# A hybrid decoder layer on one core: x loaded by columns, and the first transposes and splits ordered by k-tile

## The chip, the core and the metric

The kernel runs on one core of a Trainium2 chip. The metric is the device time of one execution in microseconds (us), the median of several runs. Times inside an execution come from a profile of one execution, counted from the start of its span.

Names of the engines: TensorE (PE, with its weight loads PEld), VectorE (DVE), ScalarE (ACT), GpSimd (POOL) and SyncE (SP), which issues most transfers.

## The reference

One decoder layer for 256 tokens with a width of 1024, all in float32: a SwiGLU feed-forward of width 2816 with RMSNorm before and after it, a mixer (state space branch and differential attention), and a second feed-forward. Only the beginning of the first feed-forward bears on the change:

```
def rmsnorm(x, g):
    y = x * lax.rsqrt(jnp.mean(x * x, axis=-1, keepdims=True) + EPS)
    return y * g

def swiglu(x, w_gate, w_up, w_down):
    return (silu(x @ w_gate) * (x @ w_up)) @ w_down

h = h + 0.5 * rmsnorm(swiglu(rmsnorm(h, ffn1_pre_g), ffn1_w_gate, ffn1_w_up, ffn1_w_down), ffn1_post_g)
```

## The kernel before, in words

Products keep close to float32 accuracy by splitting both operands into a rounded upper part (`hi`, type float32r) and a remainder (`lo`). ScalarE writes `hi` (a copy or an activation with a new type), VectorE writes `lo` as the difference, and TensorE sums three products: hi by hi, lo by hi, hi by lo.

The 256 tokens are two blocks of 128, the width of 1024 is eight k-tiles of 128. x lies in the tile `h` as 128 x 2 blocks x 1024. Weights come in chunks of 1 MB through three buffers called `raw`; each chunk is split into `whi` and `wlo`. The first four chunks hold 512 rows (four k-tiles) by 512 columns: two of `w_gate`, then two of `w_up`. The function `load_to` (line 231) issues the loads on SyncE's queue, the first chunk in four quarters of one k-tile each; a buffer is loaded again when its last split is done. `split_steps` (line 241) is a generator that issues the splits of a chunk piece by piece; the very first piece is copied by VectorE, the others by ScalarE. The first chunk's pieces are one k-tile each.

At the beginning there is no norm yet. `raised(b, q)` (line 888) transposes 512 columns (half q) of block b on TensorE, four transposes into one PSUM bank. `raw(b, q)` (line 891), through `gained` (line 473), writes hi and lo of the transposed columns times the norm's gain into the tile `raw_u` of that block and half: four activations on ScalarE, then four remainders on VectorE. The products are taken from these unnormed activations; the row factor `1 / rms` is applied later, when the sums are read. `square` (line 496) sums the squares for it, on VectorE for block 0 and on ScalarE for block 1.

`mm_both` (line 345) multiplies one chunk with both blocks: 24 products of 128 x 128 by 512 columns, six for each k-tile, in the order hi of k-tiles 0 and 1, lo of 0, hi of 2, lo of 1, hi of 3, lo of 2, lo of 3. Its argument `between` calls a function after so many products. In `first_products` (line 908) the first chunk's call puts the transposes of the second half behind products 10 and 14. The second chunk's call follows, then two more for `w_up`.

The order of TensorE, ScalarE, VectorE and SyncE is that in which the program issues the instructions here (`own_order`, line 387); each engine works its own list in order, and waits between engines are set by the tiles that are written and read. `warm(n)` (line 422) issues filler products on zeros; `FILL` is the number after the first transposes.

Order of the work before: SyncE loads block 0's first 512 columns of x, block 1's, the four quarters of the first chunk, the second 512 columns of both blocks, the second and third chunk. TensorE does five fillers, a small transpose of the gains, four transposes of block 0, a filler, four of block 1, two fillers, and the first products.

Of the kernel before, what the change touches and what calls it, by code (L numbers as in the profile page):

```python
# [16 lines left out]
F32 = mybir.dt.float32  # L17
F32R = mybir.dt.float32r
AF = mybir.ActivationFunctionType
ALU = mybir.AluOpType  # L20
# [6 lines left out]
P = 128  # L27
T = 256
# [10 lines left out]
RAW_BUFS = 3  # L39
H_PAD, ACS_PAD = 32, 0  # L40
AHEAD = 3
WARM = 5
FILL = 2
TAIL = 3
BG_US = 3.15
QK_US = 2.4
# [8 lines left out]
def tile_hybrid_layer(ctx: ExitStack, tc: tile.TileContext, x, ffn1_pre_g, ffn1_w_gate, ffn1_w_up,  # L55
# [4 lines left out]
    nc = tc.nc  # L60
# [28 lines left out]
    def bg(shape, name):  # L89
        return ps.tile(shape, F32, tag="bg", name=name, bufs=5)  # L90
# [137 lines left out]

    taken = [0]

    def load_to(n):
        while len(raws) < min(n, len(chunks)):
            i = len(raws)
            src, shape = chunks[i]
            r = sb.tile(shape, F32, tag="raw", name=f"raw{i}", bufs=RAW_BUFS)
            nj = shape[1] // 4 if i == 0 else shape[1] // 2 if i < 4 else shape[1]
            for j in range(0, shape[1], nj):
                nc.sync.dma_start(r[:, j:j + nj, :], src[:, j:j + nj, :])
            raws.append(r)

    def split_steps(ahead=True):


        i, _ = units[len(splits)]
        load_to(i + 1)
        r, shape = raws[i], chunks[i][1]
        nj = shape[1] // 2
        his, los = [], []
        splits.append((his, los))
        for q in range(2):  # L250
            hi = k4([P, nj, shape[2]], f"whi{i}{q}", F32R)
            lo = k4([P, nj, shape[2]], f"wlo{i}{q}", F32R)
            his.append(hi)
            los.append(lo)
            n = 1 if i == 0 else nj
            for j in range(0, nj, n):
                js = slice(j, j + n)
                copy = nc.scalar.copy if i + q + j else nc.vector.tensor_copy
                behind(copy(hi[:, js, :], r[:, q * nj + j:q * nj + j + n, :]), "cast")  # L259
                if not i + q + j:  # L260
                    yield
                m = nc.vector.tensor_sub(lo[:, js, :], r[:, q * nj + j:q * nj + j + n, :], hi[:, js, :].bitcast(F32))  # L262
                last_wlo[0] = behind(m, "lo").ins
                yield
        raws[i] = None
        if ahead:
            load_to(i + 1 + RAW_BUFS)
# [79 lines left out]
    def mm_both(accs, w, acts, k0, first, last, between={}):  # L347


        wh, wl = w  # L350
        his = [[(b, a, wh, j) for b in range(2) for a in acts[b]] for j in range(4)]
        los = [[(b, acts[b][0], wl, j) for b in range(2)] for j in range(4)]
        terms = his[0] + his[1] + los[0] + his[2] + los[1] + his[3] + los[2] + los[3]
        for i, (b, x_, w_, j) in enumerate(terms):
            nc.tensor.matmul(accs[b], x_(k0 + j), w_(j), start=first and j == 0 and w_ is wh and x_ is acts[b][0],  # L355
                             stop=last and j == 3 and w_ is wl)
            if i + 1 in between:
                between[i + 1]()
# [39 lines left out]
    h = const.tile([P, 2, D], F32, name="h")  # L398
    xv = x[0].rearrange("(b p) d -> p b d", p=P)
    halves = (slice(0, 512), slice(512, D))  # L400
    for q in range(2):
        for b in range(2):
            nc.sync.dma_start(h[:, b, halves[q]], xv[:, b, halves[q]])
        load_to((1, RAW_BUFS)[q])
    act_table(SILU)

    zeros = const.tile([P, P], F32, name="zeros")
# [1 line left out]
    ident = const.tile([P, P], F32, name="ident")  # L409
# [41 lines left out]
    uh, ul, _ = act_u  # L451
# [15 lines left out]
    def transposed(b, q, src, name):  # L467
        pu = bg([P, 4, P], f"pu_{name}{b}{q}")
        for i in range(4):
            nc.tensor.transpose(pu[:, i, :], src[:, i * P:(i + 1) * P], ident)  # L470
        return pu

    def gained(pu, q, g, hi, lo):

        for i in range(4):
            nc.scalar.activation(hi[:, i, :], pu[:, i, :], AF.Identity, scale=g(q * 4 + i))
        for i in range(4):
            nc.vector.scalar_tensor_tensor(lo[:, i, :], pu[:, i, :], g(q * 4 + i), hi[:, i, :].bitcast(F32),
                                           ALU.mult, ALU.subtract)
# [16 lines left out]
    def square(ss, b, q, tag, eng=None):  # L496

        src = h[:, b, halves[q]]
        if eng is nc.vector:
            nc.vector.scalar_tensor_tensor(jk([P, 512], f"sq_{tag}{b}{q}"), src, 1.0 / D, src, ALU.mult,  # L500
                                           ALU.mult, accum_out=ss[:, q:q + 1])
        else:
            sum_sq(ss[:, q:q + 1], src, 1.0, f"sq_{tag}{b}{q}")
# [26 lines left out]
    def rescaled(pus, rbs, g, tag):  # L530

        out = []
        for q in range(2):
            us = k2([P, 4, P], f"us_{tag}{q}")
            for i in range(4):
                nc.vector.scalar_tensor_tensor(us[:, i, :], pus[q][:, i, :], g(q * 4 + i), rbs, ALU.mult,
                                               ALU.mult)
# [195 lines left out]
    class Norm:  # L733
# [63 lines left out]

        def rescale(self):
            rbs = on_rows(bg([P, P], f"rb_{self.tag}"), diag(self.r0, self.tag), self.tag)
            set_u(0, rescaled(self.pus, rbs, self.g, self.tag))  # L800

    ov = out[0].rearrange("(b p) d -> p b d", p=P)

# [81 lines left out]
    pus = [[None] * 2 for _ in range(2)]  # L885
    ss_f = [tiny(2, f"ss_f{b}") for b in range(2)]

    def raised(b, q):
        pus[b][q] = transposed(b, q, h[:, b, halves[q]], "f1")

    def raw(b, q):
        gained(pus[b][q], q, gain_f, *raw_to[b](q))

    square(ss_f[0], 0, 0, "f1", nc.vector)
    raised(0, 0)
    warm(1)
    raised(1, 0)
    warm(FILL)
    steps = split_steps(False)
    next(steps)  # L900
    raw(0, 0)
    raw(1, 0)
    for _ in steps:
        pass
    square(ss_f[1], 1, 0, "f1")
    load_to(1 + RAW_BUFS)

    def first_products(evict, back):


        acts = [of_block(to) for to in raw_to]
        acc = [[pj(f"pn_f1{b}0") for b in range(2)], None]
        mm_both(acc[0], take(1), acts, 0, True, False, {10: lambda: raised(0, 1), 14: lambda: raised(1, 1)})
        square(ss_f[0], 0, 1, "f1", nc.vector)
        r = [rstd_of(ss_f[0], 1.0, "r_f10")]
        dr = diag(r[0], "f10")
        raw(0, 1)
        raw(1, 1)
        rb = bg([P, 2, P], "rb_f1")
        rbs = []  # L920
        w = take(1)
        square(ss_f[1], 1, 1, "f1")
        r.append(rstd_of(ss_f[1], 1.0, "r_f11"))
        dr1 = diag(r[1], "f11")
        us = []

        def second():
            rbs.append(on_rows(rb[:, 0, :], dr, "f10"))
            us.append(rescaled(pus[0], rbs[0], gain_f, "f10"))
# [10 lines left out]
        us = rescaled(pus[1], rbs[1], gain_f, "f11")  # L940
# [178 lines left out]
    for i in range(4):  # L1119
        acc = k2([P, 2, T], f"bc{i}")  # L1120
# [447 lines left out]
```

## Time and profile before

| what | value |
|---|---|
| median of 3 runs | 734.62 us (733.73 to 734.84) |
| span of the profiled execution | 732.0 us |
| TensorE busy | 724.0 us, 99% of the span |
| VectorE busy | 609.2 us, 83% |
| ScalarE busy | 475.3 us, 65% |
| transfers | 137.92 MB, mean 188 GB/s |

The page gives the span of the profiled execution, from the first instruction to the last; what lies around it is not in the profile, and the median of the runs is 2.62 us above the span. In the profile's rows a line such as L476 is a line of the kernel, `out<-in` names tiles with their buffer numbers left out, and a merged row (x4) gives the start of the first and the length until the end of the last. Instructions of one engine overlap a little, so that a group of four is shorter than four times the length of one.

### The profile page before, as it was taken

The numbers are of one execution on the slowest core, as the hardware profiler recorded it, in microseconds if no ns is written. First come the engines' busy times: TensorE is split into PE (matmuls) and PEld (weight loads), VectorE is DVE, ScalarE is ACT, GpSimd is POOL, SyncE is SP. The second block draws the span as 40 slices with busy tenths as digits, with TensorE's granted clock in tenths as the row PEclk, the third lists the DMA queues.
The fourth block names the chain that finished last, engine by engine and source line by source line (L and its number), as shares of the span: only waits on it lengthen the run. The fifth ranks groups of instructions, "written<-read, shape, count | busy, mean of one in ns | idle before, by whom it ended". The sixth has DMA issues, their size and how long they took to land.

```text
span 732.0 us, 10570 instructions
## 1 busy us (share of the span) xinstructions
PE 724.0 (99%) x4025; PEld 618.4 (84%) x4025; DVE 609.2 (83%) x948; ACT 475.3 (65%) x815; POOL 37.0 (5%) x66
## 2 busy tenths in 40 slices
PE   9999999999999999999999999999999999999996
PEld 7888888888878889999888888888888888888885
DVE  6978787999979999877996997784784878779995
ACT  6656566656867676869965577772663657566562
POOL 2800000000200000000000000000010000000000
PEclk9999999999999999999999999999999999999999
DMA  8874645467673647666564664475471664654541
GB/s 290 241 247 157 225 146 203 173 210 279 182 228 118 201 146 250 187 192 207 159 221 146 215 209 147 140 246 187 129 238 35 231 195 153 227 205 145 185 185 57
DMA packets 94210, 137.92 MB, mean 188 GB/s; under 512 B 2684, under 2 KB 68304, under 8 KB 94160
## 3 DMA queue, kind: packets, MB, share of 16 engines
q1 hardware_dynamic: 91488, 129.51, 53.1%
q0 software_dynamic: 2368, 7.22, 3.2%
q8 instruction: 31, 0.51, 0.3%
q10 hardware_dynamic: 304, 0.53, 0.2%
q14 instruction: 19, 0.16, 0.1%
HBM read 136.17 MB, written 1.08 MB: 188 GB/s over the span
## 4 chain that ended last, share of the span: by engine, by line
PE 99%; DVE 0%; ACT 0%; DVEq 0%; issue 0%; ACTq 0%
PE pup_f L326 9%; PE pg_f L326 9%; PE pws L345 6%; PE pgt L345 6%; PE acc_f1p L692 5%; PE acc_f2p L692 5%; PE pxs L326 4%; PE pg_f L325 4%; PE pup_f L325 4%; PE pn_f L355 3%; PE acc_mx L614 3%; PE pn_mx L345 3%; PE pn_f L345 3%; PE pwd L345 3%; PE acc_f1p L614 2%; PE acc_f2p L614 2%
## 5 line engine op out<-in xcount | busy, mean ns | idle before, releaser
L262 DVE TENSOR_TENSOR wlo<-raw,whi 128x1024 fp32r<-128x1024 f32 (+1 forms) x222 | 262.2, 1209 | 19.5 <-ACT whi L259 18.3
L259 ACT CAST whi<-raw 128x1024 fp32r<-128x1024 f32 (+1 forms) x221 | 222.8, 1043 | 12.8 <-PE psc L1255 2.5
L326 PE MATMUL pup_f<-u_f,whi 128*128 128x512 f32 x288 | 101.5, 396 | 0.0
L326 PE MATMUL pg_f<-u_f,whi 128*128 128x512 f32 x288 | 101.3, 396 | 0.0
L325 PE MATMUL pg_f<-u_f,wlo 128*128 128x256 f32 x252 | 70.6, 280 | 0.0
L325 PE MATMUL pup_f<-u_f,wlo 128*128 128x256 f32 x252 | 70.3, 279 | 0.0
L326 PEld LDWEIGHTS pup_f<-u_f,whi 128*128 128x128 f32 x288 | 52.9, 188 | 9.9
L326 PEld LDWEIGHTS pg_f<-u_f,whi 128*128 128x128 f32 x288 | 52.8, 188 | 9.7
L325 PEld LDWEIGHTS pg_f<-u_f,wlo 128*128 128x128 f32 x252 | 47.5, 189 | 1.7
L325 PEld LDWEIGHTS pup_f<-u_f,wlo 128*128 128x128 f32 x252 | 47.5, 189 | 1.6
L326 PE MATMUL pxs<-u_mx,whi 128*128 128x512 f32 x128 | 44.6, 397 | 0.0
L130 ACT CAST wqh<-wt 128x1024 fp32r<-128x1024 f32 x24 | 25.3, 1054 | 23.3 <-DVE wt L122 22.1
L330 ACT COPY su_f<-pup_f 128x256 f32<-128x256 f32 x36 | 13.4, 372 | 37.5 <-PE pup_f L326 37.4
L331 DVE TENSOR_TENSOR su_f<-pup_f,su_f 128x256 f32<-128x256 f32 x36 | 15.1, 421 | 25.0 <-ACT su_f L330 24.9
L345 PE MATMUL pgt<-whi,u_mx 128*128 128x512 f32 x128 | 33.1, 393 | 0.0
L311 PE MATMUL pz<-u_mx,whi 128*128 128x256 f32 x128 | 31.8, 285 | 0.0
L312 PE MATMUL pz<-u_mx,whi 128*128 128x256 f32 x128 | 31.4, 283 | 0.0
L325 PE MATMUL pxs<-u_mx,wlo 128*128 128x256 f32 x112 | 31.2, 279 | 0.0
L135 DVE TENSOR_TENSOR wql<-wt,wqh 128x1024 fp32r<-128x1024 f32 x24 | 29.2, 1218 | 0.2
L345 PEld LDWEIGHTS pgt<-whi,u_mx 128*128 128x128 f32 x128 | 23.6, 188 | 5.3 <-issue 0.7
L326 PEld LDWEIGHTS pxs<-u_mx,whi 128*128 128x128 f32 x128 | 23.2, 188 | 4.2
L301 ACT CAST gh_f<-sg_f 128x512 fp32r<-128x512 f32 x18 | 11.2, 620 | 23.0 <-DVE sg_f L848 23.0
(415 smaller groups left out, 1699.1 us busy)
## 6 DMA issues: line engine op xcount, KB each, us to landing
raw<-in_w_in_dram SPq DMA_DIRECT2D x40, 1024.0 KB, 5.2
raw<-in_ffn_w_down_dram SPq DMA_DIRECT2D x22, 1024.0 KB, 4.9
raw<-in_ffn_w_gate_dram SPq DMA_DIRECT2D x20, 1024.0 KB, 5.2
raw<-in_ffn_w_up_dram SPq DMA_DIRECT2D x20, 1024.0 KB, 5.2
raw<-in_ssd_w_branch_dram SPq DMA_DIRECT2D x8, 1024.0 KB, 4.9
acb<-acd POOLq DMA_DIRECT2D x8, 512.0 KB, 5.0
raw<-in_da_w_branch_dram SPq DMA_DIRECT2D x4, 1024.0 KB, 4.9
raw<-in_w_out_dram SPq DMA_DIRECT2D x4, 1024.0 KB, 4.9
```

Source lines behind the costliest of these rows:

```text
L130: nc.scalar.copy(hi, src)
L135: nc.vector.tensor_sub(lo, src, hi.bitcast(F32))
L259: behind(copy(hi[:, js, :], r[:, q * nj + j:q * nj + j + n, :]), "cast")
L262: m = nc.vector.tensor_sub(lo[:, js, :], r[:, q * nj + j:q * nj + j + n, :], hi[:, js, :].bitcast(F32))
L311: nc.tensor.matmul(acc[m], wh(j)[:, cs], ah(k0 + j), start=first and j == ks[0], stop=False)
L312: nc.tensor.matmul(acc[m], wh(j)[:, cs], al(k0 + j), start=False, stop=False)
L325: nc.tensor.matmul(acc[:, :T], wl(j)[:, cs], ah(j), start=False, stop=False)
L326: nc.tensor.matmul(acc, wh(j)[:, cs], ahl(j), start=j == 0, stop=j == KD - 1)
L345: nc.tensor.matmul(acc, a(k0 + j), b(j), start=first and i == 0, stop=last and i == 11)
L355: nc.tensor.matmul(accs[b], x_(k0 + j), w_(j), start=first and j == 0 and w_ is wh and x_ is acts[b][0], stop=last and j == 3 and w_ is wl)
L614: nc.tensor.matmul(acc[b][q][:, cs] if to is None else to, x_[:, ts], w_(kt)[:, halves[q]][:, cs], start=to is not None and kt == 0 and x_ ...
L692: nc.tensor.matmul(bank[p], x_, w_, start=p not in begun, stop=last and p in (1, 5, 6, 7))
```

## The change

x is loaded by columns: first 256 columns of both blocks in one transfer (`load_x`), then the first two quarters of the first weight chunk, then the next 256 columns of both blocks, then the other two quarters, then the rest of x by blocks as before. `load_to` has a callback for it.

`raised(n)` now transposes k-tiles 2n and 2n + 1 of both blocks (four transposes into one bank) and `raw(*ks)` writes hi and lo of whole k-tiles for both blocks. Before the first product stand the transposes of k-tiles 0 and 1 and one filler. The transposes of k-tiles 2 and 3, with their splits, the remaining splits of the first chunk and the first squares (`second_quarter`), are called after the sixth product. The transposes of k-tiles 4 and 5 and of 6 and 7 are called after products 16 and 20.

```
-FILL = 2
+FILL = 1
...
-    def load_to(n):
+    def load_to(n, half_way=None):
...
             for j in range(0, shape[1], nj):
+                if half_way is not None and j == shape[1] // 2:
+                    half_way()
                 nc.sync.dma_start(r[:, j:j + nj, :], src[:, j:j + nj, :])
...
-                if not i + q + j:
+                if i == 0:
                     yield
...
-    for q in range(2):
-        for b in range(2):
-            nc.sync.dma_start(h[:, b, halves[q]], xv[:, b, halves[q]])
-        load_to((1, RAW_BUFS)[q])
+    def load_x(cs):
+        nc.sync.dma_start(h[:, :, cs], xv[:, :, cs])
+
+    load_x(slice(0, T))
+    load_to(1, lambda: load_x(slice(T, 2 * T)))
+    for b in range(2):
+        nc.sync.dma_start(h[:, b, halves[1]], xv[:, b, halves[1]])
+    load_to(RAW_BUFS)
...
-    square(ss_f[0], 0, 0, "f1", nc.vector)
-    raised(0, 0)
-    warm(1)
-    raised(1, 0)
+    def raised(n):
+        pus[n] = pu = bg([P, 2, 2, P], f"pu_f1{n}")
+        for b in range(2):
+            for i in range(2):
+                nc.tensor.transpose(pu[:, b, i, :], h[:, b, (2 * n + i) * P:(2 * n + i + 1) * P], ident)
+
+    def raw(*ks):
+        for j in ks:
+            for b in range(2):
+                nc.scalar.activation(raw_to[b](j // 4)[0][:, j % 4, :], pus[j // 2][:, b, j % 2, :], AF.Identity,
+                                     scale=gain_f(j))
+        for j in ks:
+            for b in range(2):
+                hi, lo = raw_to[b](j // 4)
+                nc.vector.scalar_tensor_tensor(lo[:, j % 4, :], pus[j // 2][:, b, j % 2, :], gain_f(j),
+                                               hi[:, j % 4, :].bitcast(F32), ALU.mult, ALU.subtract)
+
+    raised(0)
     warm(FILL)
     steps = split_steps(False)
     next(steps)
-    raw(0, 0)
-    raw(1, 0)
-    for _ in steps:
-        pass
-    square(ss_f[1], 1, 0, "f1")
-    load_to(1 + RAW_BUFS)
+    raw(0)
+    raw(1)
+    next(steps)
+    next(steps)
+    next(steps)
+
+    def second_quarter():
+        raised(1)
+        next(steps)
+        raw(2)
+        next(steps)
+        next(steps)
+        raw(3)
+        for _ in steps:
+            pass
+        load_to(1 + RAW_BUFS)
+        square(ss_f[0], 0, 0, "f1", nc.vector)
+        square(ss_f[1], 1, 0, "f1")
...
-        mm_both(acc[0], take(1), acts, 0, True, False, {10: lambda: raised(0, 1), 14: lambda: raised(1, 1)})
+        mm_both(acc[0], take(1), acts, 0, True, False, {6: second_quarter, 16: lambda: raised(2), 20: lambda: raised(3)})
...
-        raw(0, 1)
-        raw(1, 1)
+        raw(4, 5)
+        raw(6, 7)
```

Two lines that rescale the transposed activations later (`rescaled`) take them by k-tile from the new banks; what they compute is the same.

More of the change, by code (lines that the diff above doesn't have):

```diff
@@ L535, in rescaled @@
             for i in range(4):
-                nc.vector.scalar_tensor_tensor(us[:, i, :], pus[q][:, i, :], g(q * 4 + i), rbs, ALU.mult,
+                nc.vector.scalar_tensor_tensor(us[:, i, :], pus[q][i], g(q * 4 + i), rbs, ALU.mult,
                                                ALU.mult)
@@ L799, in rescale @@
             rbs = on_rows(bg([P, P], f"rb_{self.tag}"), diag(self.r0, self.tag), self.tag)
-            set_u(0, rescaled(self.pus, rbs, self.g, self.tag))
+            set_u(0, rescaled([[pu[:, i, :] for i in range(4)] for pu in self.pus], rbs, self.g, self.tag))
     ov = out[0].rearrange("(b p) d -> p b d", p=P)
@@ L884, in tile_hybrid_layer, with of_pus @@
     gain_f = lambda j: cols_f[:, j:j + 1]
-    pus = [[None] * 2 for _ in range(2)]
+    pus = [None] * 4
     ss_f = [tiny(2, f"ss_f{b}") for b in range(2)]
[L888 to L892, printed above, removed]
-    square(ss_f[0], 0, 0, "f1", nc.vector)
-    raised(0, 0)
-    warm(1)
-    raised(1, 0)
+    def raised(n):
[3 more added lines that the diff above has]
+                nc.tensor.transpose(pu[:, b, i, :], h[:, b, (2 * n + i) * P:(2 * n + i + 1) * P], ident)
+    def of_pus(b):
+        return [[pus[2 * q + i // 2][:, b, i % 2, :] for i in range(4)] for q in range(2)]
+    def raw(*ks):
[9 more added lines that the diff above has]
+    raised(0)
     warm(FILL)
@@ L928, in second @@
             rbs.append(on_rows(rb[:, 0, :], dr, "f10"))
-            us.append(rescaled(pus[0], rbs[0], gain_f, "f10"))
+            us.append(rescaled(of_pus(0), rbs[0], gain_f, "f10"))
             ws.append(take(1))
@@ L939, in first_products @@
             evict(b, 0, acc[0][b], r[b])
-        us = rescaled(pus[1], rbs[1], gain_f, "f11")
+        us = rescaled(of_pus(1), rbs[1], gain_f, "f11")
         mm_both(acc[1], w2, acts, 0, True, False)
```

## The prediction

> **What bounds the kernel now.** I read the page first: its span, its busy times and the summary of the chain that ended last.
>
> ```profile
> span 732.0 us, 10570 instructions
> PE 724.0 (99%) x4025; PEld 618.4 (84%) x4025; DVE 609.2 (83%) x948; ACT 475.3 (65%) x815; POOL 37.0 (5%) x66
> PE 99%; DVE 0%; ACT 0%; DVEq 0%; issue 0%; ACTq 0%
> ```
>
> TensorE (PE) is busy for 724.0 of 732.0 us and the chain is TensorE nearly throughout. From the second weight chunk on, the compiled order of every engine is the same in both kernels. So what the change does to the time is what it does to the moment at which TensorE begins the second chunk's products; everything behind that moves along. The second view is the chain in order of time, at the beginning (start, length, what).
>
> ```profile
> 6.17 0.38 ACT raw_u L476
> 6.55 0.84 DVE raw_u L478 x3
> ...
> 7.59 0.35 DVE raw_u L478
> 7.98 2.10 PE pn_f L355 x7
> 10.09 0.44 PE pu_f L470 x4
> 10.52 0.93 PE pn_f L355 x4
> 11.46 0.44 PE pu_f L470 x4
> 11.89 4.29 PE pn_f L355 x18
> ```
>
> From 7.98 on the chain lies on TensorE. A product of 512 columns costs 0.93/4 = 0.233 us, four transposes 0.44. The first chunk has 24 products, six for each k-tile: four with the weights' upper part (`whi`), two with the remainder (`wlo`). I call them P1 to P24, and P25 is the second chunk's first. The third view is the timeline of the same stretch (start, length, engine, line, operation; in brackets the idle time and what ended it).
>
> ```profile
> 0.80 0.86 SPq L403 DMA_DIRECT2D h<-in_x_dram  x2
> 1.70 1.85 SPq L238 DMA_DIRECT2D raw<-in_ffn_w_gate_dram  x4
> 3.74 1.11 PE L470 MATMUL pu_f<-ident,h 128*128 128x128 f32 x4
> 4.89 2.43 ACT L476 ACTIVATE raw_u<-pu_f,cols_f 128x128 fp32r<-128x128 f32 x8 [2.20 <-PE pu_f L470]
> 5.08 1.06 PE L470 MATMUL pu_f<-ident,h 128*128 128x128 f32 x4
> 6.21 0.43 DVE L259 CAST whi<-raw 128x512 fp32r<-128x512 f32 x1 [1.59 <-DMA raw<-in_ffn_w_gate_dram]
> 6.55 2.15 DVE L478 SCALAR_TENSOR_TENSOR raw_u<-pu_f,cols_f,raw_u 128x128 fp32r<-128x128 f32 x8
> 6.78 0.94 PE L355 MATMUL pn_f<-whi,raw_u 128*128 128x512 f32 x3
> 7.19 1.68 ACT L259 CAST whi<-raw 128x512 fp32r<-128x512 f32 x3
> 7.98 1.42 PE L355 MATMUL pn_f<-whi,raw_u 128*128 128x512 f32 x5 [0.27 <-DVE raw_u L478]
> 8.62 2.49 DVE L262 TENSOR_TENSOR wlo<-raw,whi 128x512 fp32r<-128x512 f32 x4
> 9.36 0.73 PE L355 MATMUL pn_f<-wlo,raw_u 128*128 128x512 f32 x2
> 10.56 1.14 ACT L476 ACTIVATE raw_u<-pu_f,cols_f 128x128 fp32r<-128x128 f32 x4 [1.07 <-PE pu_f L470]
> 11.03 0.68 DVE L500 SCALAR_TENSOR_TENSOR sq_f<-h 128x512 f32<-128x512 f32 x1
> 11.93 1.14 ACT L476 ACTIVATE raw_u<-pu_f,cols_f 128x128 fp32r<-128x128 f32 x4 [0.23 <-PE pu_f L470]
> 12.95 2.01 ACT L259 CAST whi<-raw 128x1024 fp32r<-128x1024 f32 x2
> 13.11 1.12 DVE L478 SCALAR_TENSOR_TENSOR raw_u<-pu_f,cols_f,raw_u 128x128 fp32r<-128x128 f32 x4 [0.25 <-ACT raw_u L476]
> 14.06 1.69 PEld L355 LDWEIGHTS pn_f<-whi,raw_u 128*128 128x128 f32 x8 [0.29 <-ACT whi L259]
> 14.15 2.35 DVE L262 TENSOR_TENSOR wlo<-raw,whi 128x1024 fp32r<-128x1024 f32 x2
> 16.16 0.71 PE L355 MATMUL pn_f<-wlo,raw_u 128*128 128x512 f32 x2
> ```
>
> Two things are to be seen. First, the first product waits for the first quarter of the weights (VectorE's `whi` at 6.21, after 1.59 us of waiting for the transfer). Second, P25 at 14.06 comes right behind ScalarE's cast of the second chunk: the last four transposes end at 11.90, four casts of the activations follow at 11.93, the weights' cast at 12.95, P25 at 14.06. That chain takes 14.06 - 11.90 = 2.16 us, and the ten products between (10 x 0.233 = 2.33) just cover it. The chain's row with 18 products in 4.29 us shows that nothing is lost there.
>
> **The change part by part.** *Transfers.* x comes as 256 columns of both blocks, then half of the first weights, the next 256 columns, the other half. The first weight quarter now stands second in SyncE's queue and not third. Landing times of before (median time to landing, by the moment of issue):
>
> ```profile
> h<-in_x_dram SPq DMA_DIRECT2D x1, 256.0 KB, 2.7
> h<-in_x_dram SPq DMA_DIRECT2D x1, 256.0 KB, 3.1
> raw<-in_ffn_w_gate_dram SPq DMA_DIRECT2D x1, 256.0 KB, 4.5
> ```
>
> The first x piece lands at 0.80 + 2.7 = 3.5, the second, issued 0.43 later, at 4.33, the first weight quarter at 1.70 + 4.5 = 6.2. For the new landing of that quarter the bounds are 4.33 (the place it takes) and 6.2 (no later than before, with fewer bytes ahead). I take 5.35: the new x piece at 3.5 plus the gap of 6.2 - 4.33 = 1.87 between the last x piece and the first weights, since it is again the first weight transfer behind x. The second quarter is wanted at 6.85 (below); as the fourth piece before, it was there by ScalarE's 7.19, and it is third now. The other pieces have as many bytes ahead as before.
>
> *The chain of the first two k-tiles.* In the compiled program the remainders (`lo`, VectorE) and the casts (`hi`, ScalarE) of one activation tile wait for each other, because they write one tile. The old trace has such a wait in one direction: at 13.11 VectorE begins only after all four casts (11.93 + 1.14 = 13.07), hop 0.04. New is the other direction, since the work now alternates by k-tile: the casts of k-tile 1 wait for the remainders of k-tile 0, and behind them on ScalarE stands the cast of the second weight quarter, on which P5 depends. A pair of casts costs 0.26 + 0.37 = 0.63, a pair of remainders 0.26 + 0.34 = 0.60, by these durations (min/median/max ns) and the spacing inside the groups of four, (1.14 - 0.37)/3:
>
> ```profile
> L476 ACT ACTIVATE raw_u<-pu_f,cols_f x16: 360/368/381, 4.9 to 12.7; 128x128 fp32r<-128x128 f32 x16
> L478 DVE SCALAR_TENSOR_TENSOR raw_u<-pu_f,cols_f,raw_u x16: 340/343/353, 6.5 to 13.9; 128x128 fp32r<-128x128 f32 x16
> ```
>
> Step by step: the first four transposes end at 4.85 as before; casts of k-tile 0 from 4.89 to 5.52; VectorE's `whi` from 5.35, the next instruction 0.34 behind (6.21 to 6.55) at 5.69; remainders of k-tile 0 to 6.29; casts of k-tile 1 from 6.33 to 6.96; ScalarE's weight cast starts 0.52 after the second of them, at 6.85 (spacing of the three at 7.19), and takes 0.64 ((1.68 - 2 x 0.52)): 7.49. P5 starts at 7.53 and ends 0.50 later, as the product at 7.98 did (1.42 - 4 x 0.233): 8.03; P6 8.26. Before, P5 ended at 7.98 + 0.50 + 0.233 = 8.71. So the start gains 0.7 us up to P5, less than the 0.85 by which the weights come earlier.
>
> *Then TensorE.* The transposes of the second 256 columns now stand behind P6: 8.70. Casts of k-tile 2 to 9.37, remainders from 9.41, the first done at 9.75. P7 to P11 end at 9.87 by their number; P12 waits for that remainder: 9.79 + 0.50 = 10.29, a stall of 0.19. P13 to P16: 11.22. Third transposes: 11.66. Casts and remainders of k-tile 3 are done by 11.32 (10.05 to 10.68, then 10.72 to 11.32), in time. P17 to P20: 12.59. Last transposes: **13.03**, against 11.90.
>
> *What is late next.* The last transposes stand behind 20 products instead of 14, so that only four (0.93 us) are left to cover the 2.16 us of casts that follow. TensorE is done with P24 at 13.96 and idles; P25 comes at 13.03 + 2.16 = **15.19**, 1.13 later than 14.06.
>
> *Covered parts.* The square of block 0's first half, done by VectorE in its wait for the weights before, moves behind the splits: 0.7 us more there. The remainders of the second half then begin about 13.1; eight at 0.26 end near 15.2, and the second chunk's first `wlo` is done at 15.2 + 1.2 = 16.4. The products that need it come at 15.19 + (16.16 - 14.06) = 17.3: 0.9 of cover, nothing is lost. If VectorE were 0.9 later, it would cost one for one. SyncE's next weight load, two halves, waits for the last `wlo` of chunk 0, about 11.9 instead of 11.1 (8.62 + 2.49):
>
> ```profile
> raw<-in_ffn_w_up_dram SPq DMA_DIRECT2D x4, 512.0 KB, 6.8
> 21.35 1.05 ACT L259 CAST whi<-raw 128x1024 fp32r<-128x1024 f32 x1
> ```
>
> At 6.8 us to landing it is there by 19 to 20; its cast began at 21.35, so nothing is lost. Two fillers of TensorE go and cost nothing where they stood, in a wait; all else is the same instructions in another order.
>
> **Sum.** Up to P5 -0.68; between P8 and P9 the old wait for the first `wlo` goes (P8 ended at 9.40, P9 at 9.36 + 0.73 - 0.233 = 9.86, so -0.23 beside its own 0.233); six products and four transposes more ahead of the last transposes, 6 x 0.233 + 0.44 = +1.84; the stall at P12 +0.19: +1.12, and 1.13 by the times above. The span goes to 733.1. The runs' median (734.62) lies 2.6 above the span of the profiled execution; I take that as unchanged: **735.7 us**, +0.15%. About 0.2% (1.5 us) is what a measurement of this kernel can tell from no change.
>
> **Rivals.** *A, late weights.* The first quarter keeps its time from issue (1.23 + 4.5 = 5.73) or even its old landing, 6.2. From about 5.2 on each microsecond counts in full (before that ScalarE's casts hold the remainders): 735.7 + 0.4 to 0.85, 736.1 to 736.5. For it: the old gap of 1.87 behind x is not explained by bytes. Against: fewer bytes are ahead of it. It decides from 5.7 on. Landing at 4.33 instead would bring only 0.13, the casts being the bound: 735.6.
>
> *B, a slow array.* The granted clock is 90% or more throughout on the page:
>
> ```profile
> PEclk9999999999999999999999999999999999999999
> ```
>
> Yet four transposes took 1.11 and 1.06 us early and 0.44 later, and products were at 0.233 from 6.78 on: the array doubled its speed between 6.1 and 6.8. With two of the three fillers gone, it idles near 5.3 and again before P5; if the step came one stretch later, P6 to P16 and their transposes would go at half speed until the chain of casts is no longer what holds them: four transposes +0.44 and four products +0.93, less the 0.2 of stall at P12 and P11's wait, +1.0 to 1.1, 736.7. Against it: what runs slowly fills the gaps itself. The Trainium skill, "TensorE: Matmul & The Clock Gate", Part 1, says that the array leaves half rate after about 3.4 us of sustained activity, judged in free-running windows; the trace agrees as to the doubling, at some 5.3 us after the first filler. By that page an interrupted window would cost a further 3.4 us at half rate, which is rival B; a window counted as busy despite two short gaps leaves the sum as it is.
>
> *C, the change does what its order suggests.* If the second chunk's cast were not held by the last casts of the activations, P25 would follow P24 at once: 13.96 against an old end of P24 near 14.19 (11.89 + 10 x 0.233), 734.4; with the alternating waits cheaper than I reckon, 733.9. Against it: ScalarE takes its instructions in order, and the four casts stand ahead of the weights' cast in the compiled order.
>
> **How the numbers follow.** Forecast 0.65, A 0.15, B 0.12, C 0.08. The range runs from 734.8 (forecast less 0.4 for hops and stalls and as much for the spread of the runs) to 736.9 (B and its spread); it leaves out C. Slower by over 0.2% (beyond 736.1): B, most of A and a sixth of the forecast, 0.30. Faster by over 0.2% (below 733.15): a part of C, 0.03. Same: 0.67.
>
> **What would show it.** Right: last transposes ending near 13.0, P25 near 15.2 with an idle TensorE of over 1 us ended by ScalarE's `whi`, P5 near 7.5 waiting for ScalarE, and from there the same lengths as before. Wrong: P25 near 14 (C), the first `whi` on VectorE starting after 5.7 (A), four transposes behind P6 taking 0.8 us or more (B).

## The result, and the profile after

| | median (range), runs | ratio to before, 95% interval |
|---|---|---|
| before, beside after | 734.26 us (733.53 to 734.93), 6 | |
| after | 737.77 us (737.2 to 740.7), 6 | 1.0057 [1.0043, 1.007] |

The change makes the kernel slower by 3.5 us; forecast were 735.7 and a range up to 736.9. The profiled execution of after took 739.77 us, 2.0 above its median, so its trace shows the losses at their larger end. The page of after: its span, TensorE's busy time, and the summary of the chain that ended last.

```profile
span 738.0 us, 10565 instructions
PE 727.0 (99%) x4021; PEld 619.4 (84%) x4021; DVE 609.8 (83%) x948; ACT 475.3 (64%) x815; POOL 36.6 (5%) x66
PE 93%; DVE 3%; DMA 1%; issue 1%; ACT 1%; DVEq 0%; ACTq 0%
```

Against before's summary (PE 99%, everything else nought) the chain now leaves TensorE for 7% of the span. The chain in order of time says where (start, length, what); first its beginning, and its first long row.

```profile
0.80 3.15 DMA h<-in_x_dram
...
5.56 3.29 PE pn_f L357 x6
8.85 0.77 PE pu_f L900 x4
...
13.51 0.45 PE pu_f L900 x4
...
14.25 0.88 ACT raw_u L908 x3
15.12 0.94 ACT whi L261
...
16.11 2.12 PE pn_f L357 x8
...
20.98 12.28 PE pn_f L357 x54
```

In before the row of 54 products stood at 18.94:

```profile
18.94 12.28 PE pn_f L355 x54
```

It begins in the second chunk, behind the last row factor's product (the expectations below call it loosely the beginning of the third chunk). So the first stage ends 2.04 us later. The timeline of the same stretch, beside the rows quoted for the prediction:

```profile
4.62 0.43 DVE L261 CAST whi<-raw 128x512 fp32r<-128x512 f32 x1 [0.60 <-DMA raw<-in_ffn_w_gate_dram]
...
6.96 0.62 ACT L261 CAST whi<-raw 128x512 fp32r<-128x512 f32 x1
...
16.11 2.12 PE L357 MATMUL pn_f<-whi,raw_u 128*128 128x512 f32 x8 [1.23 <-ACT whi L261]
16.20 2.35 DVE L264 TENSOR_TENSOR wlo<-raw,whi 128x1024 fp32r<-128x1024 f32 x2
```

The idle time of 1.23 us before P25, ended by ScalarE's `whi`, is the one forecast. The six products at 5.56 and the transposes at 8.85, both at half speed, are not: that is rival B. But 2 us are not the whole. The chain has a second place where it leaves TensorE, 150 us later, at the down projection of the first feed-forward. After:

```profile
169.61 1.15 DVE wql L135
...
170.77 6.81 DMA raw<-in_ffn_w_down_dram
...
177.66 1.05 ACT whi L261
...
178.74 1.24 DVE wlo L264
...
180.02 10.98 PE acc_f1p L621 x40
191.00 0.87 PE pu_mx L477 x8
```

Before, over the same stretch:

```profile
172.66 12.30 PE acc_f1p L614 x54
184.96 1.07 PE pu_mx L470 x8
```

In before TensorE went through; in after the last load of `w_down` takes 6.81 us, and TensorE waits for its casts. The windows show the rest of the price (from and to, length, TensorE's busy time, granted clock, DMA share, GB/s):

```profile
178.00:180.00 2.00, 0.73 (x2) 1.00 1.05 409
180.00:182.00 2.00, 1.98 (x5) 0.52 0.92 358
182.00:184.00 2.00, 2.00 (x7) 0.63 0.80 214
```

TensorE idles for 1.3 and 0.5 us, and then runs at half clock, which the trace's clock record puts at 180.06 to 183.48: 3.4 us at 0.50, worth 1.7 us. The transposes for the mixer's norm (`pu_mx`) stand at 184.96 in before's chain and 191.00 in after's: 6.04 later, 2.04 from the first stage and 4.0 from this place, of which the idle time and the half clock make 3.6. At the end the spans differ by the same 6.0.

### The profile page after: what moved, and what is told of

The parts are those of the page before. It is cut to its first block, busy times and chain, and to the rows that moved or that the text cites. A ratio compares the mean times of both kernels' runs of the same rounds, so it can differ in the third digit from the quotient of the medians.

```text
span 738.0 us, 10565 instructions
## 1 busy us (share of the span) xinstructions
PE 727.0 (99%) x4021; PEld 619.4 (84%) x4021; DVE 609.8 (83%) x948; ACT 475.3 (64%) x815; POOL 36.6 (5%) x66
## 4 chain that ended last, share of the span: by engine, by line
PE 93%; DVE 3%; DMA 1%; issue 1%; ACT 1%; DVEq 0%; ACTq 0%
PE pup_f L328 9%; PE pg_f L328 9%; PE pws L347 6%; PE pgt L347 6%; PE acc_f2p L699 5%; PE pxs L328 4%; PE pg_f L327 4%; PE pup_f L327 4%; PE pn_f L357 3%; PE acc_mx L621 3%; PE pn_mx L347 3%; PE pn_f L347 3%; PE pwd L347 3%; PE acc_f2p L621 2%; PE pz L313 2%; PE pz L316 2%
```

## Why the last weights came late

The down projection takes part of its weights by quads: the four quarters of two chunks are added and subtracted by VectorE (`wt`), and the results are split into `wqh` (ScalarE) and `wql` (VectorE). Three rows, of ScalarE, GpSimd and SyncE (start, length, engine, line, operation; in brackets the wait). After:

```profile
163.89 1.05 ACT L130 CAST wqh<-wt 128x1024 fp32r<-128x1024 f32 x1 [1.50 <-DVE wt L122]
170.69 0.53 POOL L594 DMA_DIRECT2D pg_f<-in_ffn_post_g_dram  x1 [135.22 <-PE acc_f1p L699]
170.77 0.37 SPq L240 DMA_DIRECT2D raw<-in_ffn_w_down_dram  x1
```

Before:

```profile
161.44 1.05 ACT L130 CAST wqh<-wt 128x1024 fp32r<-128x1024 f32 x1 [1.21 <-DVE wt L122]
168.32 0.37 SPq L238 DMA_DIRECT2D raw<-in_ffn_w_down_dram  x1
168.65 0.53 POOL L587 DMA_DIRECT2D pg_f<-in_ffn_post_g_dram  x1 [135.22 <-PE acc_f1p L692]
```

Two transfers are issued nearly together: the last 1 MB of `w_down`, when ScalarE's and VectorE's splits free a buffer, and the post gain broadcast to 128 partitions (`pg_f`, 512 KB, `load_gain`, line 592), when TensorE frees one. In before the load went first by 0.33 us; in after the gain does, by 0.08. What then shares the DMA engines is seen by queue (q1 holds SyncE's loads, q0 GpSimd's; packets, MB, share of 16 engines), microsecond by microsecond. Before, from 171.3 and from 172.3:

```profile
q1 hardware_dynamic: 100, 0.41, 100.3%
...
q0 software_dynamic: 75, 0.31, 74.5%
q1 hardware_dynamic: 44, 0.11, 28.8%
```

After, from 173.7 and from 174.7:

```profile
q1 hardware_dynamic: 52, 0.21, 52.0%
q0 software_dynamic: 49, 0.20, 48.7%
...
q1 hardware_dynamic: 56, 0.23, 56.8%
q0 software_dynamic: 49, 0.20, 51.6%
```

With the load ahead it has the engines to itself at 0.41 MB/us until it is nearly done. With the gain ahead, the two take half each, and the load's last part goes at 0.21 to 0.23 MB/us. The Trainium skill, "DMA: Bandwidth & Descriptors", section "Queues, rings and completion order", says that each DMA engine takes turns between the queues that it has work for; these rows agree, 0.21 to 0.20 MB.

What turned the order round is mostly the 0.29 us by which ScalarE's cast of the second quad starts late: 1.50 us of waiting and not 1.21, in every profiled execution of after and of the kernels that leave its lists as they are. Counted from the start of the long row, the gain is issued at 149.71 us in both kernels, the load at 149.38 in before and at 149.79 in after: 0.41 later, the cast's 0.29 among it. In both traces the cast is released by VectorE's `wt`. What differs is its place: after's ScalarE list has one separate wait more, ahead of the first square, so that the cast is the 191st instruction and not the 190th; VectorE's list is one longer as well.

That gave the theory: two losses, a first stage longer by 2 us (the forecast's casts plus the slow array), and a collision that one more instruction in a list brings about. The rivals: the second loss is only what any later start does; the transfers are late for some other reason; and, for the first stage, the array's half speed has nothing to do with the gaps in its work.

## The experiments

**The changed kernel again**, unedited, for the spread of its trace.

> The changed kernel once more, to see whether its second loss repeats. Theory: the start costs 2.05 us (P25 at 16.11 against 14.06), of which about 0.9 is the array that stays at half speed until 9.3 us, and the rest of the 3.5 us in the median is a wait for the last weights of the first down projection that only some executions have. So P25 between 15.2 and 16.2, the span between 734 and 738, and where TensorE does not idle between 170 and 185 us the span is 734 to 735. Rival: a second loss is there in every execution of this kernel; then TensorE idles by over 1 us between 170 and 185 us again.

Measured: 739.79 us, 1.0074 [1.0052, 1.0097], beside before at 734.6, as for the next three. P25 at 16.16, P1 to P6 at half speed, and the second loss again: the load lands after 7.3 us, TensorE idles for 1.9 and 0.5 us, and the granted clock is 0.50 from 180.07 to 186.90, twice as long as in after. The four runs lie between 738.25 (mean granted clock 0.999) and 742.46 (0.993), and their median is 2.0 above that of the first six runs of the same kernel: the second loss is in both profiles of it, but its size is not the same each time.

**Fillers back.**

```
-FILL = 1
+FILL = 2
-        mm_both(acc[0], take(1), acts, 0, True, False, {6: second_quarter, ...
+        mm_both(acc[0], take(1), acts, 0, True, False, {4: lambda: warm(2), 6: second_quarter, ...
```

> The changed kernel with a second filler after the first transposes and two more behind product P4, where TensorE waits for ScalarE. Theory: the array reaches full speed by about 6.5 us as before, the four transposes behind P6 take 0.44 instead of 0.77 to 0.97 us, P25 comes near 15.2 and the time falls by 0.9 us. Rival: the half speed has nothing to do with TensorE's gaps; then the transposes still take 0.8 us and P25 stays near 16.1.

Measured: 738.64 us, 1.0052 [1.0037, 1.0067]. The transposes behind P6 are at full speed, but P25 comes at 15.76, only 0.35 earlier than in after: x landed 0.17 later in this execution and the fillers stand in the way. The second loss is there (gain issued 0.14 ahead of the load, which lands after 7.4 us): TensorE idles for 1.97 and 0.52 us, more than in after, and yet the clock stays full. The same windows as shown for after, from this run:

```profile
178.00:180.00 2.00, 0.73 (x2) 1.00 1.05 409
180.00:182.00 2.00, 1.59 (x7) 1.00 0.97 378
```

So the median, 1.15 below the unedited kernel's 739.79 beside it, doesn't show what the fillers brought at the start: the two profiles differ by the 6.8 us of half clock at 180 us as well.

**Earlier transposes.**

```
-        ... {6: second_quarter, 16: lambda: raised(2), 20: lambda: raised(3)})
+        ... {6: second_quarter, 8: lambda: raised(2), 10: lambda: raised(3)})
```

> The changed kernel with the transposes of the second half behind products 8 and 10 instead of 16 and 20. Theory: the last transposes end near 11.2 instead of 13.95, but ScalarE, which still has its casts, one square and eight casts of activations in line, begins the second chunk's cast near 14.4, so P25 near 15.4, 0.7 us earlier than 16.11. Rival: the place of the transposes is not what holds P25; then it stays at 16.1, or becomes later because the transposes wait for x (landing 9.1 to 9.7).

Measured: 738.86 us, 1.0057 [1.0042, 1.0072]. P25 comes at 14.62 (expected 15.4) and the long row begins at 19.72, 1.26 earlier than in after; the time is 0.9 below the unedited kernel's beside it, and above the 737.77 of its first runs. The second loss is there again (gain 0.09 ahead, landing 6.7 us, half clock for 3.4 us). The bound moved from the last casts to the row factor of block 1 on GpSimd.

**Before, made late** by twelve fillers.

```
-FILL = 2
+FILL = 14
```

> The kernel before with 12 more fillers (14 instead of 2) ahead of its first products, so that its start is late by about 2 us and nothing else is changed. Theory: P25 near 16.0 and the time 2 us over the kernel before, spans 734 to 735, with the wait for the down projection's last weights in a few executions at most. Rival: a late start by itself provokes the second loss; then TensorE idles between 170 and 185 us and the time is 3.2 us or more over the kernel before.

Measured: 735.8 us, 1.0015 [1.0005, 1.0024]. The long row begins at 20.72, nearly as late as in after, and there is no second loss: the load goes out 0.15 ahead of the gain and lands after 4.9 us, TensorE runs through. P25 comes at 15.84. So a late start alone costs no more than it is long: 1.2 us by the medians (0.4 to 1.8 by the interval, 2 were expected) for 1.78 us in the trace. The rest of after's loss is something else.

**After, with the gain issued later.** GpSimd first copies one column of the cast that begins behind the load, and so waits for it; the copy is overwritten by the gain.

```
         pg = k4([P, D], name)
+        if name == "pg_f1":
+            nc.gpsimd.tensor_copy(pg[:, :1], splits[taken[0]][0][0][:, 0, :1].bitcast(F32))
         nc.gpsimd.dma_start(pg, v[0].partition_broadcast(P))
```

> After the change, but GpSimd's issue of the first post gain (pg_f) follows a one-column copy of the first plain down-projection weights' cast, so that it goes out about 1 us behind the last w_down load instead of 0.1 us ahead of it; the rest is unchanged. Theory (the second loss is the collision of the 512 KB gain broadcast with the last w_down load): the load lands after some 4.8 us instead of 6.8, ScalarE's wait before the two whi casts falls from 3.2 to about 1.2 us, TensorE has no idle time at acc_f1p, its clock stays full there, and the offset against before stays at 2.0 us: 736.4 to 736.8 for before at 734.6. Rival (the loads are late for another reason, such as the later start itself): the last w_down load lands as late as in after, and the time stays at 737.8 or above.

Measured: 736.25 us (735.51 to 737.05), 1.0029 [1.0017, 1.0041], beside before at 734.44, as for all that follow but the last: 1.5 us below after. Its rows of GpSimd and ScalarE:

```profile
171.84 0.53 POOL L596 DMA_DIRECT2D pg_f<-in_ffn_post_g_dram  x1 [0.30 <-POOL pg_f L595]
175.35 1.05 ACT L261 CAST whi<-raw 128x1024 fp32r<-128x1024 f32 x1 [1.31 <-DMA raw<-in_ffn_w_down_dram]
```

The wait for the last weights is 1.31 us, where it was 3.16 in after, the load lands after 5.0, TensorE still idles for 0.32 us at `acc_f1p` (none was expected), and the clock stays at 1.00. ScalarE's cast of the second quad still waits 1.50: the collision is removed, not its cause.

**After, with one tiny ScalarE instruction more.**

```
     warm(WARM)
+    spare = const.tile([P, 1], F32, name="spare")
+    nc.scalar.copy(spare, zeros[:, :1])
```

> After the change with one tiny ScalarE copy (128x1) more, behind the first fillers at about 2 us, where ScalarE waits anyway; every later ScalarE instruction stands one place later in its list. Theory (the 0.28 us by which ScalarE's cast wqh of the second quad starts late comes from the place of that instruction in ScalarE's list, 191st against 190th, so from fetching the instructions): the wait in front of that cast falls from 1.50 to about 1.21 us, or the delay goes to a neighbour that can hide it; the last w_down load then goes out ahead of the gain broadcast, the second loss is gone and the time is 736.4 to 736.8. Rivals: it hangs on VectorE's list (250th against 249th) or on how the engines stand to each other; then the wait stays at 1.50 and the time at 737.8.

Measured: 736.12 us (735.61 to 737.52), 1.003 [1.0018, 1.0043].

```profile
163.28 1.05 ACT L130 CAST wqh<-wt 128x1024 fp32r<-128x1024 f32 x1 [1.22 <-DVE wt L122]
170.16 0.37 SPq L240 DMA_DIRECT2D raw<-in_ffn_w_down_dram  x1
170.43 0.53 POOL L596 DMA_DIRECT2D pg_f<-in_ffn_post_g_dram  x1 [135.24 <-PE acc_f1p L701]
```

The cast, now 192nd, waits 1.22 us, the load goes out 0.27 ahead of the gain, and 1.65 us of after's 737.77 are gone: an instruction more made the kernel faster.

**Before, with the same instruction.** The edit is the same.

> Before, with the same tiny ScalarE copy: its cast wqh of the second quad becomes the 191st instruction of its list, as in after. Theory (place in ScalarE's list): the wait in front of that cast rises from 1.21 to 1.50 us, the last w_down load then goes out behind the gain broadcast, lands about 2 us later and the time rises by 1.5 to 3.8 us, to 736 to 738.4. Rivals (VectorE's list, or how the engines stand to each other): 1.21 us and 734.6 as before.

Measured: 736.47 us (734.84 to 738.47), 1.003 [1.0019, 1.004].

```profile
161.82 1.05 ACT L130 CAST wqh<-wt 128x1024 fp32r<-128x1024 f32 x1 [1.50 <-DVE wt L122]
168.70 0.37 SPq L238 DMA_DIRECT2D raw<-in_ffn_w_down_dram  x1
168.72 0.53 POOL L589 DMA_DIRECT2D pg_f<-in_ffn_post_g_dram  x1 [135.21 <-PE acc_f1p L694]
```

With its cast in place 191, before shows the same wait of 1.50. The two issues fall together (0.02 us), the load lands after 6.3 us, and TensorE waits 0.7 and 0.5 us at `acc_f1p`. The second loss has been made in the kernel before, with a first stage left as it was (the long row at 19.01). Here the clock stays at 1.00.

**Before, with one VectorE instruction more** (a memset of 128x1 at the beginning).

> Before, with one tiny VectorE memset (128x1) more at the very beginning: VectorE's wql of the second quad becomes the 250th instruction of its list, as in after, while ScalarE's list stays. If the 0.28 us hang on VectorE's list, the wait in front of ScalarE's cast wqh rises from 1.21 to 1.50 us and the time by 1.5 to 3.8 us, to 736 to 738.4; if they hang on ScalarE's list or on neither, 1.21 us and 734.6.

Measured: 734.77 us (734.34 to 735.69), 1.0009 [1.0, 1.0019]. The cast waits 1.22 us, the load lands after 5.0. So it hangs on the place in ScalarE's list, not in VectorE's.

The traces show where the delay sits. A trace also has the separate waits among ScalarE's records, and counts one more than the compiled list, so that the cast is record 191 in before and 192 in after. In the seven profiles where it is record 192 (after, again, fillers, early_turns, after_pg_late, before_act1, and turns_pg_late below) it starts 0.32 us behind the wait ahead of it; where it is record 191 or 193, 0.04. With the cast at 191, record 192 is a wait that follows the running cast: that wait starts 0.30 to 0.32 us behind the cast's start, where after's starts 0.02 behind. So in before, too, the 192nd record is late by about 0.3 us, but a running cast hides it. In the two kernels whose first stage is put in another order further below (squares_early, squares_dense) the cast is back at 191 and waits 1.22.

Sorted by how far the load's issue is ahead of the gain's, the traces form one row:

| kernel | load ahead by, us | load's issue to landing, us |
|---|---|---|
| after_pg_late | 1.52 | 5.0 |
| before | 0.33 | 4.8 |
| after_act1 | 0.27 | 5.2 |
| before_dve1 | 0.20 | 5.0 |
| before_late | 0.15 | 4.9 |
| before_act1 | 0.02 | 6.3 |
| after | -0.08 | 6.8 |
| early_turns | -0.09 | 6.7 |
| fillers | -0.14 | 7.4 |
| again | -0.14 | 7.3 |

In the four kernels with the late gain that follow, the load is 1.53 us ahead and lands after 4.9.

**Both mended: early transposes and the late gain.** The two edits shown above, together.

> After with two edits together: the last two transposes (raised(2), raised(3)) behind products 8 and 10 in place of 16 and 20, as in the run of that edit alone, and the gain broadcast behind the last w_down load. Theory (two losses that add: the later end of the first stage, and the collision at the down projection): the third chunk's products begin some 0.8 us later than in before, nothing is lost at the down projection, and the whole stands 0.8 us above before: 735.2 for before at 734.4. Rival (the collision was only one of several ways in which a shifted start costs time later): over 736.

Measured: 736.47 us (735.43 to 737.57), 1.0024 [1.0015, 1.0033]. A miss by over 1 us, at the rival's figure, though there was no collision (the load landed after 4.9 us). The same order of the first stage gave two different stages. TensorE's rows of the run with earlier transposes alone, and then of this one:

```profile
5.45 1.61 PE L357 MATMUL pn_f<-whi,raw_u 128*128 128x512 f32 x4 [0.24 <-ACT raw_u L908]
8.08 0.60 PE L900 MATMUL pu_f<-ident,h 128*128 128x128 f32 x4
```

```profile
5.91 3.29 PE L357 MATMUL pn_f<-whi,raw_u 128*128 128x512 f32 x6
9.00 1.05 PE L902 MATMUL pu_f<-ident,h 128*128 128x128 f32 x4
```

By the clock records the array is at full speed from 4.84 us in the first and from 10.19 in the second, and the long row begins at 19.72 and at 21.06. So the gain that I had read off the first run was mostly the array's speed in that execution. Of the six profiled executions so far that have after's fillers, two were at full speed below 6 us (early_turns and after_pg_late), and after, again, after_act1 and this one only from 8.5 to 10.2.

**The order of the first stage mended** (with the late gain).

```
-        ... {6: second_quarter, 16: lambda: raised(2), 20: lambda: raised(3)})
+        ... {6: second_quarter, 10: lambda: raised(2), 12: lambda: raised(3)})
...
         raised(1)
+        square(ss_f[1], 1, 0, "f1")
         next(steps)
+        square(ss_f[0], 0, 0, "f1", nc.vector)
         raw(2)
...
         load_to(1 + RAW_BUFS)
-        square(ss_f[0], 0, 0, "f1", nc.vector)
-        square(ss_f[1], 1, 0, "f1")
...
-        w = take(1)
         square(ss_f[1], 1, 1, "f1")
+        w = take(1)
```

> After with the order of the first stage mended as its trace points: the last two transposes behind products 10 and 12; the squares of the first 512 columns of both blocks in the idle time of ScalarE and VectorE ahead of the third weights quarter; the last square of block 1 ahead of the second chunk's casts; and the gain broadcast behind the last w_down load. Theory (TensorE itself bounds the first stage once no cast, transpose or row factor makes it wait): the third chunk's products begin at 18.8 to 19.3 us against 18.94 in before, and the time is 734.3 to 734.9, the same as before. Rival (x by columns costs the stage time by itself: half clock for the first products and casts in smaller pieces): the third chunk still begins at 19.7 or later, 735.2 or more.

Measured: 735.82 us (734.88 to 736.68), 1.0016 [1.0007, 1.0024]; the long row at 20.11. Both figures are the rival's (19.7 or later, 735.2 or more), and the trace has P1 to P6 at half speed, as the rival says (3.28 us for six; full speed from 9.02). Whether columns of x must cost this is what the last run tells.

**Before, with the late gain.**

> Before with the gain broadcast behind the last w_down load by the same one-column copy as in the run of after. Theory (in before the broadcast already went out 0.3 us behind the load and cost TensorE nothing): 734.4, within 0.1% of before. Rival (the broadcast also slows the load in before, in part or in some of its runs): faster by 0.3 us or more, and a narrower spread of the runs.

Measured: 734.68 us (734.25 to 736.28), 1.0005 [0.9996, 1.0014]. Nothing to gain there. In its trace the transposes for the mixer's norm wait 0.8 us for VectorE:

```profile
172.40 7.90 DMA raw<-in_w_in_dram
...
186.40 1.32 PE L470 MATMUL pu_mx<-ident,h 128*128 128x128 f32 x8 [0.82 <-DVE h L583]
```

The gain itself is there in time (issued at 170.44, landed 5.9 us later, first used at 182.60). What is late is the next load behind it, of `w_in`: 7.9 us to landing, where before's two loads have a median of 5.7. VectorE stands 0.98 us waiting for that chunk's cast, and the norm behind it in VectorE's list is late by it. The later gain has moved the collision to another load, so this edit can cost as well.

**The mended order, with the gaps filled.**

```
-FILL = 1
+FILL = 2
...
+    warm(1)
     raised(0)
     warm(FILL)
```

> The kernel with the mended order (squares_early) and two fillers more on TensorE: one ahead of the first transposes, where the array waits 0.5 us for x, and one behind them, where it waits for the first operands. Theory (the array goes to full speed only behind a stretch of some 3.4 us without a gap; after's two short gaps at 3.8 and 5.8 us reset that in most executions): the first products are at full speed from 8.5 us at the latest instead of 9.0 to 9.7, the third chunk begins some 0.5 us earlier on the average than the 20.1 us of squares_early, and the time is 735.2 to 735.5 for before at 734.4. Rival (the speed of the array doesn't hang on these gaps): the third chunk at 20.1 to 20.6, 735.8 to 736.3, the fillers standing in the way of the transposes by up to 0.3 us.

Measured: 734.64 us (734.42 to 735.28), 1.0007 [0.9998, 1.0016], beside before at 734.3. TensorE's rows:

```profile
5.19 0.68 PE L432 MATMUL warm<-zeros 128*128 128x128 f32 x4
5.85 1.61 PE L357 MATMUL pn_f<-whi,raw_u 128*128 128x512 f32 x4
```

The array is at full speed from the first product on (from 5.34 us), the long row begins at 19.60, 0.5 earlier as expected, and the time is 1.2 us below the kernel without the two fillers (1.0 when each is taken against its own before), more than the 0.3 to 0.6 expected; its slowest run (735.28) is below the other's median. This kernel loads and splits x by columns as the change does, and is level with before. None of the twelve kernels beats before.

**The clock records of all 14 profiles** say more than the one profile of the last kernel. Each trace keeps the granted clock as stretches with a start, and the first begins where TensorE goes to full speed (at 6.43 us in before, between the 6.1 and 6.8 that the prediction read off the rows); the page's PEclk row takes the time ahead of it as full, and so showed none of this. All stretches but the cut one at the end are whole multiples of 3.413 us long, so the clock changes only at steps of that length. Where the steps lie differs from one execution to the next. TensorE's first filler starts at 1.11 us in every profile, so the first step with 3.4 us of work ahead of it falls somewhere between 4.5 and 7.9 us.

| TensorE ahead of that step | profiles | full speed from, us |
|---|---|---|
| idle for at most 0.1 us | before, before_late, before_dve1, before_act1, before_pg_late, fillers, squares_dense, early_turns | 6.43, 6.61, 6.55, 7.39, 7.43, 7.69, 5.34, 4.84: at that step |
| idle for 0.2 to 0.5 us, mostly waiting for x | after, again, after_act1, turns_pg_late, squares_early | 9.40, 9.41, 8.45, 10.19, 9.02: one step of 3.41 later |
| idle for 0.3 us, waiting for x | after_pg_late | 5.22: at that step |

All eight with next to no gap took the first step; of the six with a gap, five missed it. In squares_dense the step also fell early, so that its 5.34 is in part luck; without a gap it could have been up to 7.9. Why after_pg_late, idle for longer than after, did not miss its step stays open.

The same steps decide the half clock at the down projection. The step ahead of it held 1.87 us of idle time in after, 1.88 in again and 1.79 in early_turns, and half clock followed; in before_act1 it held 1.27, and in fillers the 2.5 us fell on two steps with 1.18 and 1.31, and the clock stayed full.

## Why the prediction was wrong, point by point

- **The chain of the first two k-tiles: right.** Forecast for ScalarE's second weights cast 6.85, measured 6.96; VectorE's first `whi` came at 4.62 rather than 5.35, which brought nothing, since the casts were the bound, as rival A's last sentence had it. x's first piece landed after 3.15 us and not 2.7, so that the transposes ended at 5.10 and not 4.85.
- **What is late next: right.** From the end of the last transposes to P25: 16.11 - 13.96 = 2.15, forecast 2.16; TensorE's idle time ended by `whi`: 1.23. The 1.13 us of the sum are in the trace.
- **The array's speed: rival B, weighed too low.** P6 ended at 8.85 (forecast 8.26) and the transposes behind it took 0.77 us (0.44): +0.59 and +0.33, that is 0.92; the last transposes ended at 13.96 and not 13.03, the same 0.93. I gave B 0.12 and argued that slow work fills the gaps itself. The runs show that in the new order the moment of full speed varies from 4.84 to 10.19 us. In after it came at 9.40, one step of 3.41 us behind 5.98. The gap was not quite where B had it: it is the wait for x ahead of the first transposes, which the forecast put at nothing by taking x's landing as 2.7 us (3.1 to 3.5 in the traces of the new order). Filling the gaps went with a time 1.0 to 1.2 us lower. The clock records fit the rule that the prediction cites for rival B from the Trainium skill, "TensorE: Matmul & The Clock Gate", Part 1, free-running windows of about 3.4 us: steps of 3.413 us, and a further one when the first is missed.
- **The step that failed:** "From the second weight chunk on, the compiled order of every engine is the same in both kernels", therefore "everything behind that moves along". The order was the same; the place in ScalarE's list was not. 0.29 us at one cast did most to turn two issues round, the load of the last weights took 2 us longer, TensorE idled 1.9 us and ran at half clock for 3.4. By the medians this is 1.5 to 1.65 us of the 3.5 (after less after_pg_late, after less after_act1); by the second set of runs of the unedited kernel, 739.79, it would be 3.5 or more, so its size is known only between these. Without it, after stands at 736.1 to 736.3, between the forecast of 735.7 and rival B's 736.7.
- **Covered parts: right.** The squares, VectorE's remainders (`wlo` at 16.20, forecast 15.2 plus the slow array) and the later halves of the second chunk cost nothing of their own.

What stays open: why the 191st place costs 0.28 us. That the place decides is shown both ways (192nd: gone; 191st in before: there), and in all 14 traces by which record is late. That it is the fetching of instructions is a guess; their transfers (the queues q8 and q14) didn't tell the kernels apart.

## What to carry to other kernels

A tuned kernel can depend on which of two transfers of different queues goes out first, by 0.3 us; before calling everything behind a change "unchanged", look for pairs of issues that stand that close and belong to different engines, because a single instruction more can turn them round. When a change moves a kernel by about a microsecond, compare the offset of the two traces at several places along the span, not only at the edit: here 2 us stood at 20 us and 6 at 190. And before a gain or loss is put down to the order of the work, see at which speed the array ran in that very execution: the same kernel came out 2 us apart in two sets of runs.

## What the runs showed of the hardware

- A 1 MB load lands after 4.8 to 5.2 us when a 512 KB broadcast of GpSimd is issued 0.15 us or more behind it, and after 6.3 to 7.4 us when the two are issued together or the broadcast is ahead.
- The 192nd of ScalarE's records starts about 0.3 us late in the 13 profiles that can show it (in after_act1 it falls into a wait of 2.2 us). A tiny ScalarE copy at 2 us, which moves every later instruction by one place, so changed the wait of a ScalarE cast at 162 us by 0.28 us, in both directions.
- The granted clock of TensorE changed only at steps of 3.413 us, whose place differed from one execution to the next. At the down projection, a step with 1.79 to 1.88 us of idle time (after, again, early_turns) was followed by one or two steps at 0.50; steps with 1.18 to 1.31 us (fillers, before_act1) were not.
- Going to full speed at the start asked for more: an idle time of 0.2 to 0.5 us in the step ahead put it off by one step in five of six profiles.
